# One adaLN part of a diffusion block is multiplied and summed by VectorE instead of TensorE

## The chip, the core and the metric

The kernel runs on one core of a Trainium2 chip. The metric is the device time of one execution in microseconds. The engines are named as in the profile: PE is TensorE, PEld its weight load, DVE is VectorE, ACT is ScalarE, POOL is GpSimd, and SP is the engine whose queue issues nearly all loads from memory.

## The reference, cut to what matters

One block with two sub-layers works on 256 latent tokens and 256 context tokens of width 2048. Each sub-layer is modulated by adaLN: a vector `c` goes through silu and one large matrix, and the result is cut into six vectors of 2048.

```python
def ada_modulation(cond, w, b):
    m = jax.nn.silu(cond) @ w + b          # w: 2048 x 12288
    return jnp.split(m[..., None, :], N_MOD, axis=-1)

sh_a, sc_a, g_a, sh_m, sc_m, g_m = ada_modulation(c, w_ada[layer], b_ada[layer])
h = modulate(rms_norm(x, norm_attn_w), sh_a, sc_a)      # h * (1 + scale) + shift
q, k, v, u = split_projection(h @ w_in)                 # the input projection
...                                                     # rotary, windowed attention, pooling mixer
x = x + g_a * (concat([attn, pool]) @ w_out)
hm = modulate(rms_norm(x, norm_mlp_w), sh_m, sc_m)      # needs sh_m and sc_m
x = x + g_m * squared_relu_mlp(hm, w_up, w_down)
```

The change touches how the first 256 columns of `sc_m` and the first 256 of `sh_m` are computed. They are first read by the MLP, long after the place where they are computed.

## The kernel before, in words

All weights pass once through five buffers `raw` of 128 x 4 x 512 floats (1 MB each). `WeightStream` loads them on SP's queue in a fixed order, each as soon as its buffer is free. There are two kinds of tile. A weight tile ("w") is split in two halves: ACT casts a half to `hi` (L97), DVE subtracts to get `lo` (L98), and PE multiplies in three products (L288 to L290). An adaLN tile ("ada") is read as it lies: its 512 columns are 256 of a scale and 256 of a shift, and four tiles (kg = 0 to 3) cover the 2048 rows of the sum.

The program runs through stages: the first norm, the input projection in five groups of rows, the attention with the pooling mixer beside it, the output projection, the second norm and the MLP. A scheduler with a model of the time chooses each engine's order; every engine then works through its own order strictly.

The adaLN parts that are needed late are spread over these stages. `ADA_LATE` (L32 to L36) lists twelve of them with the engine for each, four steps a part. The first entry, `("m", 0)`, has its four steps in the last group of the input projection (`LATE_IN` = 4), between the products for the values (`ps_v`) and those for the queries (`ps_qu`).

There are two ways to do a part. With "pe" (`ada_pe`) a step is four matmuls (L305), each of 32 columns of `c_sil` against 512 columns of the tile, into a bank `ps_ada`; after the fourth step ACT copies the bank to `ada_e` (L311). With "dve" (`ada_dve`) a step is four VectorE operations over 128 x 512: each multiplies a slice of the tile by a scalar per partition and adds what is there so far (L327; the very first only multiplies, L325). In both ways a finishing step then sums over partitions by small matmuls (`ada_cols`) and adds bias and weight (L340 to L344).

Around the place of the change stand these steps. The last products of the input projection are added to `ka`, `va`, `qa` and `ua` by DVE (L436). Keys and queries are rotated: DVE shuffles a copy (L634), POOL multiplies the copy and the original by the rope table (L635, L636), DVE adds the two (L637). Keys are split by ACT and DVE (L647 to L650). Queries are split for a pair of heads: ACT casts to `qs` (L659), DVE subtracts (L660). The attention works in 16 units; a unit's scores are three matmuls for each of two heads (L717 to L720), its maxima are DVE's (L728 to L730), its exponentials ACT's (L736), and the division is DVE's and ACT's (L740 to L744). The four `ua` groups (`u2` and `u3` of the last input group) are still multiplied between the first units.

Of the kernel before, what the change touches and what calls it, by code (L numbers as in the profile page):

```python
# [8 lines left out]
F32 = mybir.dt.float32  # L9
# [6 lines left out]
P = 128  # L16
# [13 lines left out]


ADA_LATE = (  # L32
    ("m", 0, "pe"), ("m", 1, "pe"),
    ("g", 0, "pe"), ("g", 1, "pe"), ("g", 2, "pe"), ("g", 3, "pe"),
    ("m", 2, "dve"), ("m", 3, "dve"), ("m", 4, "dve"), ("m", 5, "pe"), ("m", 6, "dve"), ("m", 7, "dve"),
)  # L36
# [88 lines left out]
def kernel(  # L125
# [10 lines left out]
    const = ctx.enter_context(tc.tile_pool(name="const", bufs=1, side="left"))  # L136
# [131 lines left out]
    def rstd(pool, ss, n, rest=EPS):  # L268

        nv = pool.tile([P, n], F32, tag="rs_v", name="rs_v", bufs=2)  # L270
        y = pool.tile([P, n], F32, tag="rs_y", name="rs_y", bufs=2)
        u = pool.tile([P, n], F32, tag="rs_u", name="rs_u", bufs=2)
        nc.vector.tensor_scalar(nv, ss, 1.0 / D, rest, ALU.mult, ALU.add)
        nc.vector.tensor_scalar(u.bitcast(I32), nv.bitcast(I32), 1, None, ALU.logical_shift_right)
        nc.vector.tensor_scalar(y.bitcast(I32), u.bitcast(I32), -1, 0x5F3759DF, ALU.mult, ALU.add)
        nc.vector.tensor_scalar(nv, nv, -0.5, None, ALU.mult)
        for _ in range(3):
            for c_ in range(n):
                yc, uc = y[:, c_ : c_ + 1], u[:, c_ : c_ + 1]
                nc.vector.scalar_tensor_tensor(uc, yc, nv[:, c_ : c_ + 1], yc, ALU.mult, ALU.mult)  # L280
            for c_ in range(n):
                yc, uc = y[:, c_ : c_ + 1], u[:, c_ : c_ + 1]
                nc.vector.scalar_tensor_tensor(yc, uc, 1.5, yc, ALU.add, ALU.mult)
        return y
# [30 lines left out]
    def ada_dve(finish):  # L315

        box = {}

        def step(kg):
            raw = S.next("ada")  # L320
            for j in range(4):
                sc = c_sil[:, 4 * kg + j, 0:1]
                if kg == 0 and j == 0:
                    box["e"] = mp.tile([P, 512], F32, tag="ada_v", name="ada_v", bufs=1)
                    nc.vector.tensor_scalar(box["e"], raw[:, j, :], sc, None, ALU.mult)  # L325
                else:
                    nc.vector.scalar_tensor_tensor(box["e"], raw[:, j, :], sc, box["e"], ALU.mult, ALU.add)  # L327

        return [lambda kg=kg: step(kg) for kg in range(4)] + [lambda: finish(box["e"])]

    def ada_cols(e, weights):

        ps = bank("ps_adac")
        for j in range(4):
            nc.tensor.matmul(ps[:, 2 * j : 2 * j + 2], e[:, 128 * j : 128 * j + 128], weights, start=True, stop=True)
        return ps[:, 0:8].rearrange("p (j s) -> p j s", s=2)
# [177 lines left out]
    def late_steps():  # L514
        for what, j, engine in ADA_LATE:
            ada, weights, spread = (ada_pe, sel, selb) if engine == "pe" else (ada_dve, ones[:, 0:2], ones)

            def finish(e, what=what, j=j, weights=weights, spread=spread):
                if what == "m":
                    k = slice(2 * j, 2 * j + 2)  # L520
                    ps = ada_cols(e, weights)
                    ada_scale(am[:, k], ps[:, 0:2], bcol[:, 64 + 2 * j : 66 + 2 * j], cols[:, 48 + 2 * j : 50 + 2 * j])
                    ada_shift(sm[:, k], ps[:, 2:4], bcol[:, 48 + 2 * j : 50 + 2 * j])
                else:
                    ps = bank("ps_g")
                    nc.tensor.matmul(ps, spread, e, start=True, stop=True)
                    gs = gate["a"][:, 512 * j : 512 * j + 512]
                    nc.vector.tensor_tensor(gs, ps, gs, ALU.add)

            steps = ada(finish)  # L530
            yield from steps[:4]
            late_finish.append(steps[4])
# [290 lines left out]
    mp = ctx.enter_context(tc.tile_pool(name="mp", bufs=1, side="right", reuse_waits="tile"))  # L823
# [150 lines left out]
    for b in range(7):  # L974
        acts = early[0:2] if b == 0 else [early[2], up_group()] if b == 1 else [up_group(), up_group()]
        steps = ada_dve(lambda e, b=b: gate_m_chunk(b, e)) if b < 4 else None
        for dg in range(4):
            pss = down_group(b, dg, acts)
            for i in range(2):
                accumulate(y[dg][:, i, :], pss[i], b == 0)  # L980
            if steps:
                steps[dg]()
                if dg == 3:
                    steps[4]()
# [29 lines left out]
    def finish(i, ts, last):  # L1014

        n = 3 + len(ts)
        nc.vector.tensor_reduce(mean[:, i : i + 1], ss3[:, i, 0:n], axis=AX.X, op=ALU.add)
        nc.vector.tensor_scalar(mean[:, i : i + 1], mean[:, i : i + 1], 1.0 / D, EPS, ALU.mult, ALU.add)
        ts.append(last())
        r = rstd(yp, ss3[:, i, n : n + 1], 1, mean[:, i : i + 1])  # L1020
        w = D - 1536
        for h, t in enumerate(ts):
            s = slice(1536 + w // len(ts) * h, 1536 + w // len(ts) * (h + 1))
            nc.vector.scalar_tensor_tensor(x2[:, i, s], t, r, fw[:, s], ALU.mult, ALU.mult)
        for q, eng in ((3, nc.sync), (0, nc.sync), (1, nc.scalar), (2, nc.sync)):
            xs = x2[:, i, 512 * q : 512 * q + 512]
            if q < 2 or q == 2 and i == 0:
                nc.scalar.activation(xs, xs, AF.Copy, scale=r)
            elif q == 2:
                nc.vector.tensor_scalar(xs, xs, r, None, ALU.mult)  # L1030
            eng.dma_start(out=out[P * i : P * i + P, 512 * q : 512 * q + 512], in_=xs)
# [70 lines left out]
```

## Time and profile before

| | us |
|---|---|
| median of 3 runs | 1147.65 |
| lowest and highest run | 1146.72, 1148.39 |
| the profiled execution | 1147.05 |
| its span in the trace | 1145.3 |
| PE busy in the span | 1104.6 (96%) |
| DVE busy | 779.2 (68%) |
| ACT busy | 523.6 (46%) |
| POOL busy | 37.0 (3%) |

The profiled execution took 1.75 us more than its span, and lies 0.60 us under the median. The busy shares are averages over stages with different limits: which engine is late at the place of the change has to be read there.

### The profile page before, as it was taken

What the parts mean: (1) busy time and instruction counts of PE and PEld (TensorE: products, weight loads), DVE (VectorE), ACT (ScalarE), POOL (GpSimd) and SP (SyncE); (2) the same over time, 40 slices, a digit from 0 to 9 for tenths busy, and PEclk for the clock granted to TensorE, in tenths of its full rate; (3) what the DMA queues carried; (4) which work ended last, traced back from release to release, by engine and by line L of the source; (5) the groups of instructions that cost most, each with busy time, mean ns of one, the idle gap of its engine ahead of it and who ended that gap; (6) DMA issues with size and microseconds to landing.
All of it is one profiled execution on the core that took longest, in us unless ns stands there. A gap on an engine that the chain in (4) does not pass through costs nothing.

```text
span 1145.3 us, 16131 instructions
## 1 busy us (share of the span) xinstructions
PE 1104.6 (96%) x6364; PEld 909.3 (79%) x6364; DVE 779.2 (68%) x1222; ACT 523.6 (46%) x796; POOL 37.0 (3%) x53
## 2 busy tenths in 40 slices
PE   4999999999999989999999999999999999999996
PEld 2767778856588869888888888888888888888885
DVE  4655567875588988696774874884664565587576
ACT  4633233499734343365343443433444443443452
POOL 1000001610000000000000000000000000000000
PEclk9999999999999989899999999999999999999998
DMA  9999898687799989977775776775566556566532
GB/s 343 359 341 336 288 325 264 210 292 259 267 369 314 325 306 332 336 246 259 262 265 184 257 269 195 253 267 192 184 192 202 194 184 185 191 192 204 184 110 75
DMA packets 174013, 286.66 MB, mean 250 GB/s; under 512 B 5608, under 2 KB 72352, under 8 KB 172784
## 3 DMA queue, kind: packets, MB, share of 16 engines
q1 hardware_dynamic: 172800, 279.55, 72.9%
q0 software_dynamic: 848, 5.55, 1.3%
q8 instruction: 50, 0.82, 0.3%
q10 hardware_dynamic: 288, 0.52, 0.1%
q14 instruction: 27, 0.22, 0.1%
HBM read 283.50 MB, written 2.10 MB: 249 GB/s over the span
## 4 chain that ended last, share of the span: by engine, by line
PE 88%; DVE 4%; ACT 3%; DMA 3%; issue 1%; SPq 0%; ACTq 0%; DVEq 0%
PE ps_up L919 25%; PE ps_d L288 10%; PE ps_d L289 10%; PE ps_d L290 10%; PE ps_ada L305 4%; PE ps_w L288 3%; PE ps_w L290 3%; PE ps_w L289 3%; PE ps_qu L288 2%; PE ps_qu L290 2%; PE ps_qu L289 2%; PE ps_up L288 1%; DVE lo L98 1%; PE ps_o L763 1%; PE ps_up L289 1%; PE ps_up L290 1%
## 5 line engine op out<-in xcount | busy, mean ns | idle before, releaser
L98 DVE TENSOR_TENSOR lo<-raw,hi 128x1024 fp32r<-128x1024 f32 x330 | 397.7, 1226 | 211.8 <-ACT hi L97 201.0
L97 ACT CAST hi<-raw 128x1024 fp32r<-128x1024 f32 x330 | 338.1, 1050 | 409.1 <-PE ps_up L919 151.7
L919 PE MATMUL ps_up<-mx,hi 128*128 128x512 f32 x832 | 200.1, 393 | 0.0
L288 PE MATMUL ps_d<-hi,ahi 128*128 128x512 f32 (+1 forms) x520 | 200.0, 386 | 0.0
L289 PE MATMUL ps_d<-lo,ahi 128*128 128x512 f32 (+1 forms) x520 | 200.0, 386 | 0.0
L290 PE MATMUL ps_d<-hi,alo 128*128 128x512 f32 (+1 forms) x520 | 198.7, 386 | 0.0
L919 PEld LDWEIGHTS ps_up<-mx,hi 128*128 128x128 f32 x832 | 153.4, 188 | 31.8 <-issue 1.9
L290 PEld LDWEIGHTS ps_d<-hi,alo 128*128 128x128 f32 x520 | 97.7, 188 | 19.8
L288 PEld LDWEIGHTS ps_d<-hi,ahi 128*128 128x128 f32 x520 | 97.7, 188 | 19.5
L289 PEld LDWEIGHTS ps_d<-lo,ahi 128*128 128x128 f32 x520 | 97.7, 188 | 19.3
L919 PEld LDWEIGHTS ps_up<-mx,lo 128*128 128x128 f32 x832 | 106.7, 191 | 4.0
L327 DVE SCALAR_TENSOR_TENSOR ada_v<-raw,c_sil,ada_v 128x512 f32<-128x512 f32 x135 | 100.9, 748 | 12.7 <-DMA raw<-in_w_ada_dram 11.1
L919 PE MATMUL ps_up<-mx,lo 128*128 128x256 f32 x832 | 107.9, 283 | 0.0
L288 PE MATMUL ps_qu<-hhi,hi 128*128 128x256 f32 x240 | 69.3, 290 | 1.4 <-ACT hi L97 1.4
L305 PE MATMUL ps_ada<-raw,c_sil 128*32 128x512 f32 x480 | 68.3, 628 | 2.2 <-DMA raw<-in_w_ada_dram 1.9
L290 PE MATMUL ps_qu<-hhi,lo 128*128 128x256 f32 x240 | 67.0, 282 | 0.3 <-DVE lo L98 0.3
L289 PE MATMUL ps_qu<-hlo,hi 128*128 128x256 f32 x240 | 66.9, 280 | 0.0
L288 PEld LDWEIGHTS ps_qu<-hhi,hi 128*128 128x128 f32 x240 | 45.1, 188 | 16.6 <-issue 8.4
L288 PE MATMUL ps_up<-mx,hi 128*128 128x256 f32 x192 | 54.7, 293 | 1.8 <-ACT mx L884 1.5
L289 PE MATMUL ps_up<-mx,hi 128*128 128x256 f32 x192 | 54.3, 287 | 0.0
L290 PE MATMUL ps_up<-mx,lo 128*128 128x256 f32 x192 | 53.1, 287 | 0.4 <-DVE lo L98 0.4
L288 PE MATMUL ps_w<-hi,mx 128*128 128x512 f32 x128 | 50.4, 395 | 0.0
(202 smaller groups left out, 1336.4 us busy)
## 6 DMA issues: line engine op xcount, KB each, us to landing
raw<-in_w_ada_dram SPq DMA_DIRECT2D x128, 512.0 KB, 7.3
raw<-in_w_mlp_up_dram SPq DMA_DIRECT2D x64, 1024.0 KB, 5.5
raw<-in_w_mlp_down_dram SPq DMA_DIRECT2D x64, 1024.0 KB, 5.1
raw<-in_w_ada_dram SPq DMA_DIRECT2D x32, 1024.0 KB, 6.8
raw<-in_w_in_dram SPq DMA_DIRECT2D x19, 1024.0 KB, 7.6
raw<-in_w_out_dram SPq DMA_DIRECT2D x16, 1024.0 KB, 7.5
xnat<-in_x_dram SPq DMA_DIRECT2D x2, 1024.0 KB, 6.0
xnat<-in_ctx_dram SPq DMA_DIRECT2D x2, 1024.0 KB, 11.7
```

The lines of the kernel that those rows point to most:

```text
L97: up = nc.scalar.copy(hi, raw)
L98: low = nc.vector.tensor_tensor(lo, raw, hi.bitcast(F32), ALU.subtract)
L288: nc.tensor.matmul(ps, a[0], b[0], start=first, stop=False, skip_group_check=True)
L289: nc.tensor.matmul(ps, a[0], b[1], start=False, stop=False, skip_group_check=True)
L290: nc.tensor.matmul(ps, a[1], b[0], start=False, stop=last, skip_group_check=True)
L305: nc.tensor.matmul(ps[32 * j : 32 * j + 32, :], c_sil[:, 4 * kg + j, :], raw[:, j, :], start=(kg == 0), stop=(kg == 3), tile_position=(0, ...
L327: nc.vector.scalar_tensor_tensor(box["e"], raw[:, j, :], sc, box["e"], ALU.mult, ALU.add)
L763: nc.tensor.matmul(ps[64 * i : 64 * i + 64, 0:T], va[k // 2][:, k % 2, 64 * g : 64 * g + 64], pT[:, k, i, :], start=(k == 0), stop=(k == 3 ...
L919: nc.tensor.matmul(ps, wk, h, start=part == k == 0, stop=part == 1 and k == KC - 1, skip_group_check=True)
```

## The change

The first entry of `ADA_LATE` goes from "pe" to "dve". Its sixteen products and sums are issued on DVE in place of sixteen matmuls on PE. The pool `mp`, where `ada_dve` keeps its sum, isn't open yet at this place, so the constant tile `ada_e` is used there. The copy of the bank by ACT goes; the sum over partitions uses `ones` in place of `sel`.

```diff
 ADA_LATE = (
-    ("m", 0, "pe"), ("m", 1, "pe"),
+    ("m", 0, "dve"), ("m", 1, "pe"),
...
                 if kg == 0 and j == 0:
-                    box["e"] = mp.tile([P, 512], F32, tag="ada_v", name="ada_v", bufs=1)
+                    if mp:
+                        box["e"] = mp.tile([P, 512], F32, tag="ada_v", name="ada_v", bufs=1)
+                    else:
+                        box["e"] = const.tile([P, 512], F32, tag="ada_e", name="ada_e", bufs=1)
                     nc.vector.tensor_scalar(box["e"], raw[:, j, :], sc, None, ALU.mult)
...
         return [lambda kg=kg: step(kg) for kg in range(4)] + [lambda: finish(box["e"])]
+
+    mp = None
```

Lines from L326 on stand three lines further down in the changed kernel, and those from L329 on five: the multiplying step L325 and the adding step L327 are L328 and L330 there, and the accumulation L436 is L441.

The scheduler orders the engines anew. On DVE, at the end of the input projection, this stands before, from the rotation of the second query block (`qa_272`) to the maxima of the first unit; `qa_271` to `qa_274` are the four query blocks, `qs_2108` and `qs_2111` the split queries of the first two heads, which the first two units read, and `lo` belongs to the tile that `u3` multiplies:

```order
L634 STREAM_SHUFFLE rot<-qa_272 128x2x256
L637 TENSOR_TENSOR qa_271<-qa_271,rot 128x512
L98 TENSOR_TENSOR lo<-raw,hi 128x1024 x2
L660 TENSOR_TENSOR qs_2108<-qa_271,qs_2108 64x256
L436 TENSOR_TENSOR qa_273<-ps_qu,qa_273 128x512
L660 TENSOR_TENSOR qs_2111<-qa_271,qs_2111 64x256
L660 TENSOR_TENSOR qs_2166<-qa_271,qs_2166 64x256
L637 TENSOR_TENSOR qa_272<-qa_272,rot 128x512
L660 TENSOR_TENSOR qs_2169<-qa_271,qs_2169 64x256
L634 STREAM_SHUFFLE rot<-qa_273 128x2x256
L436 TENSOR_TENSOR qa_274<-ps_qu,qa_274 128x512
L728 TENSOR_REDUCE st<-ps_s 128x1 x2
```

and now, in the same place (`qs_2106` and `qs_2109` are the split queries of the first two heads here):

```order
L330 SCALAR_TENSOR_TENSOR ada_e<-raw,c_sil,ada_e 128x512
L441 TENSOR_TENSOR qa_274<-ps_qu,qa_274 128x512
L639 STREAM_SHUFFLE rot<-qa_272 128x2x256
L639 STREAM_SHUFFLE rot<-qa_273 128x2x256
L642 TENSOR_TENSOR qa_271<-qa_271,rot 128x512
L330 SCALAR_TENSOR_TENSOR ada_e<-raw,c_sil,ada_e 128x512
L639 STREAM_SHUFFLE rot<-qa_274 128x2x256
L665 TENSOR_TENSOR qs_2106<-qa_271,qs_2106 64x256
L330 SCALAR_TENSOR_TENSOR ada_e<-raw,c_sil,ada_e 128x512
L665 TENSOR_TENSOR qs_2109<-qa_271,qs_2109 64x256
L665 TENSOR_TENSOR qs_2164<-qa_271,qs_2164 64x256
L642 TENSOR_TENSOR qa_272<-qa_272,rot 128x512
```

The last four adding steps of the part stand among the rotation and the splitting of the queries (the fourth of them follows two rows further down), and the shuffles of `qa_273` and `qa_274` and the accumulation of `qa_274` have moved ahead of the first split queries. POOL's order is the same: four products of 128 x 256 for the keys and eight of 128 x 512 for the queries, each pair behind its shuffle.

On PE, among the products for the values, this stands before:

```order
L290 MATMUL ps_v<-hi,hlo 128x256
L288 MATMUL ps_v<-hi,hhi 128x256
L289 MATMUL ps_v<-lo,hhi 128x256
L290 MATMUL ps_v<-hi,hlo 128x256
L305 MATMUL ps_ada<-raw,c_sil 32x512 x4
L288 MATMUL ps_v<-hi,hhi 128x256
L289 MATMUL ps_v<-lo,hhi 128x256
```

and now:

```order
L290 MATMUL ps_v<-hi,hlo 128x256
L288 MATMUL ps_v<-hi,hhi 128x256
L289 MATMUL ps_v<-lo,hhi 128x256
L290 MATMUL ps_v<-hi,hlo 128x256
L288 MATMUL ps_v<-hi,hhi 128x256
L289 MATMUL ps_v<-lo,hhi 128x256
```

The four matmuls of a step are gone, at this and at three more places, and the products around them are in the order that they had.

## Rows read from the trace of the kernel before

**Rows 1.** The page's part 4: shares of the chain that ended last.

```profile
PE 88%; DVE 4%; ACT 3%; DMA 3%; issue 1%; SPq 0%; ACTq 0%; DVEq 0%
```

**Rows 2.** Windows: start:end, length, busy of each engine, granted clock, DMA share, GB/s.

```profile
173.40:206.40 33.00, 33.00 (x249) 27.84 (x248) 26.16 (x42) 14.21 (x21) 9.51 (x8) 1.00 0.84 276
206.40:212.70 6.30, 5.36 (x41) 4.99 (x41) 6.11 (x13) 0.00 (x0) 2.16 (x2) 1.00 0.94 318
212.70:230.00 17.30, 17.30 (x131) 13.36 (x129) 14.25 (x33) 11.25 (x27) 13.65 (x18) 1.00 0.39 129
230.00:280.00 50.00, 46.95 (x325) 27.57 (x324) 34.33 (x92) 47.23 (x115) 4.07 (x5) 1.00 0.73 258
408.00:414.70 6.70, 6.70 (x34) 2.34 (x37) 6.67 (x20) 3.31 (x8) 0.00 (x0) 0.50 0.41 123
```

**Rows 3.** Timeline of PE around the first step: start, length, then the idle time before.

```profile
187.32 0.28 PE L290 MATMUL ps_v<-hi,hlo 128*128 128x256 f32 x1
187.53 1.06 PE L305 MATMUL ps_ada<-raw,c_sil 128*32 128x512 f32 x8
...
188.75 0.28 PE L289 MATMUL ps_v<-lo,hhi 128*128 128x256 f32 x1
```

**Rows 4.** Timeline of PE at the first scores, and behind a later stall.

```profile
206.87 0.50 PE L717 MATMUL ps_s<-khi,qs 128*128 128x512 f32 x1 [0.46 <-DVE qs L660]
...
208.13 0.47 PE L717 MATMUL ps_s<-khi,qs 128*128 128x512 f32 x1 [0.48 <-DVE qs L660]
...
208.74 0.33 PE L288 MATMUL ps_qu<-hhi,hi 128*128 128x256 f32 x1
...
221.35 0.22 PE L720 MATMUL ps_s<-mask_r,ident_r 128*128 128x128 f32 x1
...
407.11 0.70 PE L868 MATMUL ps_r<-diag,ones 128*128 128x256 f32 x2 [2.92 <-DVE diag L866]
```

**Rows 5.** Timeline of DVE from the query weights to the third unit's maxima.

```profile
194.81 2.36 DVE L98 TENSOR_TENSOR lo<-raw,hi 128x1024 fp32r<-128x1024 f32 x2 [0.45 <-ACT hi L97]
...
201.20 0.69 DVE L637 TENSOR_TENSOR qa<-qa,rot 128x512 f32<-128x512 f32 x1
202.54 3.83 DVE L98 TENSOR_TENSOR lo<-raw,hi 128x1024 fp32r<-128x1024 f32 x2 [0.65 <-ACT hi L97]
...
207.57 0.87 DVE L660 TENSOR_TENSOR qs<-qa,qs 64x256 fp32r<-64x256 f32 x2
...
212.72 0.37 DVE L729 SCALAR_TENSOR_TENSOR st<-st,nsink 128x2 f32<-128x2 f32 x1
...
224.22 1.28 DVE L728 TENSOR_REDUCE st<-ps_s 128x1 f32<-128x512 f32 x2
225.54 1.05 DVE L729 SCALAR_TENSOR_TENSOR st<-st,nsink 128x2 f32<-128x2 f32 x1
```

**Rows 6.** Timeline of POOL: products of the rotation, and one of the pooling mixer.

```profile
199.88 1.28 POOL L636 TENSOR_TENSOR qa<-qa,rope 128x512 f32<-128x512 f32 x1
201.22 1.83 POOL L635 TENSOR_TENSOR rot<-rot,rope 128x512 f32<-128x512 f32 x1
203.01 2.28 POOL L636 TENSOR_TENSOR qa<-qa,rope 128x512 f32<-128x512 f32 x1
...
225.49 1.09 POOL L671 TENSOR_TENSOR win<-win 128x538 f32<-128x538 f32 x1
```

**Rows 7.** Timeline of DVE in the output projection, where parts are already DVE's.

```profile
351.92 0.75 DVE L327 SCALAR_TENSOR_TENSOR ada_v<-raw,c_sil,ada_v 128x512 f32<-128x512 f32 x1
352.58 1.22 DVE L98 TENSOR_TENSOR lo<-raw,hi 128x1024 fp32r<-128x1024 f32 x1
```

**Rows 8.** Timeline of SP: loads of the part's four tiles, two for each.

```profile
162.38 4.38 SPq L84 DMA_DIRECT2D raw<-in_w_ada_dram  x4
...
169.77 5.49 SPq L84 DMA_DIRECT2D raw<-in_w_ada_dram  x4
```

**Rows 9.** Timeline of ACT in the third and fourth unit.

```profile
225.67 1.34 ACT L744 ACTIVATE p<-p,st 128x512 f32<-128x512 f32 x2 [2.66 <-DVE st L741]
```

## The prediction

> **What bounds the kernel now.** I read the chain that ended last first: PE holds 88% of it and DVE 4% [rows 1]. That says that removed PE work is time gained where PE leads, and it doesn't say where that is. So I cut the place of the change into windows [rows 2]. From 173.40 to 206.40, the end of the input projection, PE is busy for 33.00 of 33.00 us. DVE is busy for 26.16 us there, so 6.84 us of it are free. From 206.40 to 212.70 the order of things turns: DVE is busy for 6.11 of 6.30 us and PE for 5.36. PE's two waits there are for DVE's splits of the first queries, 0.46 and 0.48 us [rows 4]. So before the change the two engines come to the first scores almost together, DVE a little later. From 212.70 to 230.00 PE leads again (17.30 of 17.30), and from 230.00 ACT (47.23 of 50.00, PE 46.95).
>
> **What is removed.** Four steps of four matmuls leave PE. Around the first step the products for the values go from 187.32 to 188.75 [rows 3]. Two products in a row without a step between take about a quarter of a microsecond of that, so a step costs 1.2 us and four cost 4.8. The three other steps look the same. PE would then stand at the first scores at about 201.6 in place of 206.4. ACT's copy of the bank goes too; ACT is busy for 14.21 of 33.00 us up to 206.40 [rows 2], nothing waits behind it, and I count it at nothing.
>
> **What is added, without contention.** The part is sixteen operations of 128x512 on DVE. Where the kernel already has them, one starts 0.66 us before the operation behind it [rows 7]. In the new order fifteen of the sixteen stand ahead of the second split of queries, on which PE's second scores wait. Fifteen times 0.66 is 9.9 us; the very first only multiplies and may be a little cheaper, which I leave. Two shuffles and one accumulation move ahead of that split as well. I take 0.69 us for each, from the addition of the same size [rows 5], together 2.1. So 12.0 us more must pass through DVE's queue before PE can go on.
>
> Against it stand 6.84 us of free time [rows 2]. I let all of it be filled, which is generous, since some of it is time in which DVE waits for PE or ACT and will wait again. Before the change DVE also lost time at 202.54, where two subtractions took 3.83 us in place of 2.36 at 194.81 [rows 5]; those 1.5 us I take out here, because I count such losses by themselves below. So without contention the split ends 12.0 - 6.8 - 1.5 = 3.7 us later. It ended at about 208.0, half way through the row at 207.57 [rows 5]; now at 211.7.
>
> That is already the main finding. PE comes 4.8 us earlier to a point at which it must wait until a time that is later than before. The 4.8 us turn into waiting.
>
> **What is added by contention.** At 201.20 an addition on DVE and a product on POOL begin together. The product takes 1.83 us, where the one before took 1.28 [rows 6], and its end at 203.05 is that of a product that began when the addition was over (201.20 + 0.69). Then the two subtractions of DVE and the next product meet: DVE loses 1.5 us and the product takes 2.28. They take turns, whole instructions at a time. A tiny operation shows it too: the scalar-tensor-tensor of 128x2 took 1.05 us at 225.54, while a sum on POOL ran from 225.49 to 226.58 [rows 5, 6]; alone it took 0.37.
>
> In the old order few of DVE's operations met a product. In the new one DVE has no gaps, so every product that falls ahead of the second split of queries costs its length, unless DVE is at an operation which reads only one operand from SBUF (a shuffle, or an accumulation from PSUM). By the order on POOL and DVE, seven of the query products fall there: two for each of three query blocks and the first of the fourth, since the four shuffles now stand ahead. Seven times 1.28 is 9.0 us; one accumulation and two shuffles lie beside them, 2.1 off: 6.9. The four key products are half the size, 0.64 each, 2.6 together; an accumulation and a small operation hide 0.8 of it: 1.8. So contention costs 8.7 us and the split ends at 220.4, 12.4 later than before.
>
> The bounds of this term are nothing (no turns between the adding steps and POOL) and 11.6 us (each of the eleven products in full). I take 8.7, because the rows nearest to it, subtraction and addition of the same kind of operands, show turns each time they meet.
>
> No row shows an adding step of this size beside a POOL product. The Trainium skill (SBUF — State Buffer, section "SBUF: two separate sides") has one pair of ports that VectorE and GpSimd share, held for a whole instruction, and a VectorE instruction with two SBUF inputs is among those that hold it. By that rule, with which the subtraction at 202.54 agrees, the adding steps take turns with the rope products; without it the time would be that of the first rival below. It speaks against putting this part beside the rotation.
>
> **What becomes of the delay.** Three things follow. First, PE restarts 12.4 us late. Second, some of it is taken back: the third unit's scores were done on PE at 221.57 [rows 4], but its maxima started on DVE only at 224.22 [rows 5], and ACT was idle for 2.66 us there [rows 9]. With PE later, DVE has done its work by then, so I take 2.7 us off. Third, PE's clock. After an idle time of 2.92 us that ended at 407.11 [rows 4] the granted clock was 0.50 (1.2 of 2.4 GHz) over 408.00 to 414.70 [rows 2]: 6.7 us at half speed, 3.35 us of work lost. The new idle time is longer, about 10 to 19 us. PE leads after it until ACT takes over, so I count half, 1.7 us, with nothing and 3.35 as the ends. Sum: 12.4 - 2.7 + 1.7 = 11.4.
>
> **Transfers.** SP's order stays, but the buffers of the part's four tiles come free by DVE's steps in place of PE's. All four tiles' loads were issued between 162.38 and 175.26 [rows 8], ahead of nearly all of DVE's steps, so those hardly wait for data. The load that takes the last tile's buffer starts up to 16 us later than before (about 222 in place of 206). Its reader on PE stands 11 us later as well and several products behind; I count nothing, with up to 4 us if that cover is gone. Nothing is queued on SP that is read sooner. In the stages behind, PE leads and the delay passes to the end.
>
> **The sum.** 1147.05 for the profiled execution plus 11.4 is 1158.45. That execution lies 0.60 under the median, so I forecast 1159.0, slower.
>
> **Rivals.**
>
> The adding steps don't take turns with POOL, and only subtractions and additions do. For it: no row shows such a step of this size beside a POOL product. Against it: the tiny one at 225.54. In the order, an adding step stands opposite to three query products and about two key products, some 5 us of the 8.7. The split then ends at 215.4, 7.4 later; 7.4 - 2.7 + 1.7 = 6.4, so 1154.1.
>
> No contention at all, or a scheduler's order in which the products happen to fall beside accumulations: 3.7 us at the split. With 2.7 taken back and half the clock's loss that is +2.7, 1150.3; where the clock costs nothing it is +1.0, 1148.6. This is also the case in which the change is not seen.
>
> The other side: DVE's queue has room and PE's 4.8 us reach the end, 1142.9. It decides if the second split of queries ends before 203.3, that is 4.8 earlier than now. DVE's free time up to there would have to hold all 12 us, and it has 6.84. What speaks for it is only that later stages take back more than I see: the units are led by ACT from 230.00 on, where PE is idle for 3.05 of 50 us [rows 2]. That isn't enough to take back 12.
>
> **Chances.** The forecast with contention: 0.60. The first rival: 0.12. No contention: 0.18, of which 0.09 is within 0.2%. The faster one: 0.07. A larger delay, from a late tile or a longer loss at the lower clock: 0.03. About 0.2% (2.3 us) is what a measurement of this kernel can tell from no change. So faster 0.07, within it 0.09, slower 0.84. The range runs from 1148.5, which keeps the most part of the case without contention, to 1163.5, which is 12.4 us and the clock's 3.35 with nothing taken back (1147.65 + 15.75 = 1163.4).
>
> **What would show it right or wrong.** In the changed profile PE should come to the first scores near 201.6, and wait there for DVE's split of queries, in two waits that sum to between 10 and 19 us. DVE should have almost no idle time from 176 on until the first maxima. Some adding steps among the rotations should take about 1.3 us more than 0.75, or POOL's rope products more than 1.28. The granted clock should be 0.50 for a few microseconds behind the wait. The third unit's maxima should follow their scores at once. I am wrong if PE's wait at the scores is under 4.8 us (then the change gains), if the adding steps beside POOL's products keep their 0.75 us (then the first rival holds), or if PE is late by 12 us at 230 and on time at 400 (then a later stage has slack that I didn't find).

## The result and the profile after

| | before | after |
|---|---|---|
| median of the runs beside each other, us | 1148.02 (4 runs) | 1158.74 (4 runs) |
| the same, measured again | 1147.16 (17 runs) | 1160.92 (5 runs) |
| ratio, 95% interval | | 1.0102 [1.0079, 1.0125] |
| the same, measured again | | 1.0115 [1.0092, 1.0138] |
| profiled execution, and its span | 1147.05, 1145.3 | 1162.85, 1161.1 |

The change costs 1.0 to 1.2%, 11 to 14 us. Executions of one kernel differ by 3 to 10 us here, and the profiled one of the changed kernel is the longest of its four; a second profile (run "after_again") has a span of 1157.4 us. Up to the end of the attention the two agree within 0.4 us, so the rows below are from the first, and stages behind are compared with the second too.

The windows of the changed kernel, to be set beside [rows 2] (the same columns):

```profile
173.40:206.40 33.00, 27.98 (x217) 26.70 (x216) 32.44 (x53) 12.24 (x16) 7.93 (x6) 0.96 0.82 274
206.40:212.70 6.30, 0.00 (x0) 0.00 (x0) 6.30 (x10) 1.61 (x4) 4.36 (x4) 0.50 0.49 166
212.70:230.00 17.30, 14.25 (x93) 12.54 (x94) 14.74 (x26) 5.47 (x11) 9.95 (x11) 0.77 0.23 71
230.00:280.00 50.00, 47.27 (x327) 28.98 (x326) 34.49 (x89) 43.47 (x105) 9.86 (x13) 1.00 0.80 287
```

In the first window DVE (the third of the five engines) went from 26.16 to 32.44 us of 33.00, and PE fell from 33.00 to 27.98. In the second DVE has no gap, PE does nothing, and the granted clock is 0.50.

The timeline of PE at the first scores, to be set beside [rows 4]:

```profile
213.99 0.79 PE L722 MATMUL ps_s<-khi,qs 128*128 128x512 f32 x1 [12.61 <-DVE qs L665]
...
217.07 0.80 PE L722 MATMUL ps_s<-khi,qs 128*128 128x512 f32 x1 [1.76 <-DVE qs L665]
...
218.20 0.52 PE L288 MATMUL ps_qu<-hhi,hi 128*128 128x256 f32 x1
...
421.27 1.22 PE L873 MATMUL ps_r<-diag,ones 128*128 128x256 f32 x2 [2.91 <-DVE diag L871]
```

PE was ready at 201.4 and waited 12.61 and 1.76 us for DVE's splits of queries. The second scores start at 217.07 in place of 208.13.

DVE's timeline in that wait, and POOL's (beside [rows 5] and [rows 6]); L330 is the adding step, L641 and L640 are the rope products:

```profile
205.91 1.75 DVE L330 SCALAR_TENSOR_TENSOR ada_e<-raw,c_sil,ada_e 128x512 f32<-128x512 f32 x1
...
210.78 1.75 DVE L330 SCALAR_TENSOR_TENSOR ada_e<-raw,c_sil,ada_e 128x512 f32<-128x512 f32 x1
...
213.97 1.65 DVE L330 SCALAR_TENSOR_TENSOR ada_e<-raw,c_sil,ada_e 128x512 f32<-128x512 f32 x1
215.65 2.79 DVE L665 TENSOR_TENSOR qs<-qa,qs 64x256 fp32r<-64x256 f32 x2
...
219.64 0.75 DVE L330 SCALAR_TENSOR_TENSOR ada_e<-raw,c_sil,ada_e 128x512 f32<-128x512 f32 x1
```

```profile
204.86 2.24 POOL L641 TENSOR_TENSOR qa<-qa,rope 128x512 f32<-128x512 f32 x1
...
210.27 1.71 POOL L641 TENSOR_TENSOR qa<-qa,rope 128x512 f32<-128x512 f32 x1
...
213.62 1.45 POOL L641 TENSOR_TENSOR qa<-qa,rope 128x512 f32<-128x512 f32 x1
215.03 1.71 POOL L640 TENSOR_TENSOR rot<-rot,rope 128x512 f32<-128x512 f32 x1
```

The step at 205.91 ends at 207.66, 0.56 us behind the end of the product that began at 204.86. The one at 219.64 meets no product and takes 0.75. Two splits that took 0.87 us before [rows 5] take 2.79.

The third unit, to be set beside its scores and maxima in [rows 4] and [rows 5]:

```profile
231.89 0.22 PE L725 MATMUL ps_s<-mask_r,ident_r 128*128 128x128 f32 x1
...
233.20 0.68 DVE L733 TENSOR_REDUCE st<-ps_s 128x1 f32<-128x512 f32 x1
```

The times of a trace count from its first instruction, and the runs don't reach the place of the change equally soon. A step of DVE that stands ahead of the change in every run, the bias of an earlier part (`am_a`), shows it, here before, after and in the run short_rope below:

```profile
173.46 0.16 DVE L340 TENSOR_TENSOR am_a<-ps_adac,bcol 128x4 f32<-128x4 f32 x1
...
173.51 0.16 DVE L345 TENSOR_TENSOR am_a<-ps_adac,bcol 128x4 f32<-128x4 f32 x1
...
172.43 0.16 DVE L363 TENSOR_TENSOR am_a<-ps_adac,bcol 128x4 f32<-128x4 f32 x1
```

Over all runs it starts between 172.26 and 173.85. The difference is there long before the change (an accumulation into `ka` starts at 95.29 before and at 94.27 in short_rope), so no edit makes it. Delays are therefore counted from this step.

The delay along the program, from the profiles (`am_a`; start of the second scores; ACT's table load ahead of the first exponentials; the last wait of the attention's products on PE; the second norm's `ps_r`; the end):

| run | `am_a` | second scores | first exponentials | end of attention | second norm | span |
|---|---|---|---|---|---|---|
| before | 173.46 | 208.13 | 213.17 | 306.48 | 407.11 | 1145.3 |
| after | 173.51 | 217.07 | 222.94 | 318.46 | 421.27 | 1161.1 |
| after_again | 173.85 | 217.39 | 223.26 | 318.81 | 419.45 | 1157.4 |

Counted from `am_a`, the delay is 8.9 us at the second scores, 9.7 at the exponentials, 11.9 at the end of the attention, and 12 (14 in the longer execution) at the second norm. Up to the end of the attention the two profiles of the changed kernel agree within 0.03 us. At the end nothing of the delay is given back.

### The profile page after: what moved, and what is told of

The parts are those of the page before. It is cut to its first block, busy times and chain, and to the rows that moved or that the text cites. A ratio compares the mean times of both kernels' runs of the same rounds, so it can differ in the third digit from the quotient of the medians.

```text
span 1161.1 us, 16079 instructions
## 1 busy us (share of the span) xinstructions
PE 1104.3 (95%) x6332; PEld 910.8 (78%) x6332; DVE 793.6 (68%) x1238; ACT 523.5 (45%) x795; POOL 39.7 (3%) x53
## 4 chain that ended last, share of the span: by engine, by line
PE 72%; DVE 11%; DMA 11%; ACT 4%; issue 2%; SPq 1%; ACTq 0%; DVEq 0%
PE ps_up L924 25%; PE ps_d L289 10%; PE ps_d L290 10%; PE ps_d L288 10%; DMA raw<-in_w_out_dram 4%; DMA raw<-in_w_mlp_up_dram 4%; PE ps_ada L305 4%; DVE lo L98 3%; DVE ada_v L330 2%; PE ps_qu L288 2%; PE ps_qu L290 2%; DMA raw<-in_w_ada_dram 2%; PE ps_qu L289 2%; ACT hi L97 1%; PE ps_o L768 1%
## 5 line engine op out<-in xcount | busy, mean ns | idle before, releaser
L330 DVE SCALAR_TENSOR_TENSOR ada_v<-raw,c_sil,ada_v 128x512 f32<-128x512 f32 x135 | 100.9, 747 | 21.2 <-DMA raw<-in_w_ada_dram 19.7
L305 PE MATMUL ps_ada<-raw,c_sil 128*32 128x512 f32 x448 | 64.4, 625 | 1.8 <-DMA raw<-in_w_ada_dram 1.8
```

What stands on the lines that cost most here:

```text
L305: nc.tensor.matmul(ps[32 * j : 32 * j + 32, :], c_sil[:, 4 * kg + j, :], raw[:, j, :], start=(kg == 0), stop=(kg == 3), tile_position=(0, ...
```

## The experiments

Where an edit says "order kept", a table of ranks holds DVE, ACT, POOL and PE to a given order by edges that make no engine wait for another; so an edit changes durations and not the order.

```python
own = [i for i in traced if str(i.engine) == "EngineType." + name]
line = [own[a + k] for a, n in runs for k in range(n)]
for first, then in zip(line, line[1:]):
    tc.add_manual_dep(then, first.name, mybir.DependencyInfo(mybir.DependencyClass.NoSync, mybir.DependencyReason.DATA), reason="order")
```

How much later than in the kernel before each run is, in us, counted from `am_a` (in the kernel before the three places are 34.7, 133.0 and 233.7 us behind it):

| run | `am_a` | second scores | end of attention | second norm |
|---|---|---|---|---|
| after_again | 173.85 | 8.9 | 11.9 | 11.9 |
| short_rope | 172.43 | 2.1 | 6.4 | 6.4 |
| short_steps | 172.69 | 5.0 | 8.8 | 8.9 |
| both | 172.54 | 9.7 | 13.1 | 14.3 |
| short_pe | 172.66 | 0.3 | 1.0 | 1.0 |
| keep_warm | 173.10 | 9.2 | 12.2 | 13.4 |
| later_order | 173.03 | 0.1 | 6.0 | 7.2 |
| former_order | 172.26 | 8.9 | 11.4 | 11.4 |
| late_former | 172.44 | 1.3 | 8.5 | 8.5 |
| short_both | 172.39 | -0.9 | -0.7 | 0.9 |

**The changed kernel again** (after_again), no edit.

> The changed kernel once more, as the measure for the others: 1158.7, ratio 1.0102. In its profile PE restarts the products of u2 9 to 10 us later than in the kernel before, and the difference at the end is 10 to 12 us.

Measured: 1160.92 us, 1.0115. The second scores are 8.9 us late, a little less than expected. The difference at the end is 13.8 us between medians, more than expected, with the first measurement's 10.7 inside the spread.

**Short rope products** (short_rope): the changed kernel, order kept.

```diff
-        nc.gpsimd.tensor_tensor(tmp, tmp, rope[:, 1:2, :].broadcast_to([P, n, T]), ALU.mult)
-        nc.gpsimd.tensor_tensor(t, t, rope[:, 0:1, :].broadcast_to([P, n, T]), ALU.mult)
+        few = slice(0, 8)
+        nc.gpsimd.tensor_tensor(tmp[:, :, few], tmp[:, :, few], rope[:, 1:2, few].broadcast_to([P, n, 8]), ALU.mult)
+        nc.gpsimd.tensor_tensor(t[:, :, few], t[:, :, few], rope[:, 0:1, few].broadcast_to([P, n, 8]), ALU.mult)
```

> The changed kernel, every engine in its order, but POOL's rope products run over 16 of 512 columns (that part of the rotation is left out). Theory (DVE's queue and the turns with POOL): DVE's second split of queries ends about 8 us earlier than in the changed kernel, PE restarts the products of u2 near 210.5 in place of 218.2, and the time falls from 1158.7 to about 1150 to 1152. Rival (no turns; DVE is late by its own work alone, the long operations beside POOL are an artefact of the records): PE restarts within 2 us of 218.2 and the time stays at 1157 to 1159.

Measured: 1154.04 us, 1.0061 [1.0048, 1.0074]. The timeline of PE:

```profile
207.91 0.80 PE L741 MATMUL ps_s<-khi,qs 128*128 128x512 f32 x1 [7.62 <-DVE qs L684]
...
209.17 0.79 PE L741 MATMUL ps_s<-khi,qs 128*128 128x512 f32 x1
```

and of DVE:

```profile
206.02 0.74 DVE L348 SCALAR_TENSOR_TENSOR ada_e<-raw,c_sil,ada_e 128x512 f32<-128x512 f32 x1
...
207.89 0.77 DVE L348 SCALAR_TENSOR_TENSOR ada_e<-raw,c_sil,ada_e 128x512 f32<-128x512 f32 x1
208.69 0.87 DVE L684 TENSOR_TENSOR qs<-qa,qs 64x256 fp32r<-64x256 f32 x2
```

The adding steps, of full size, are back at 0.75 us and the two splits at 0.87; the second scores start 6.8 us earlier than in after_again, counted from `am_a`. The sum of what DVE's operations up to the split on which these scores wait took longer in the changed kernel than here is 6.8 us too; 3.8 us of it fall on five adding steps, the rest on subtractions, an addition and the splits. So the turns with POOL are shown, and their size at this place was 6.8 against 8.7 in the sum. The time is 2 us above the 1150 to 1152 expected: of the 6.8 us 5.6 are left at the end of the attention; where the rest went is the matter of the order runs below.

**Short adding steps** (short_steps): the changed kernel, order kept.

```diff
-                    nc.vector.scalar_tensor_tensor(box["e"], raw[:, j, :], sc, box["e"], ALU.mult, ALU.add)
+                    few = slice(0, 512 if mp else 8)
+                    nc.vector.scalar_tensor_tensor(box["e"][:, few], raw[:, j, few], sc, box["e"][:, few], ALU.mult, ALU.add)
```

> The changed kernel, every engine in its order, but fifteen of the sixteen adding steps run over 8 of 512 columns (that part of the sum is left out). Theory: with the steps' time gone DVE keeps only the moved shuffles and accumulation (2 us) and their turns with POOL, PE restarts at 207 to 210 and the time is 1146 to 1150, about that of the kernel before; PE's 4.8 us still don't come through. Rival 1 (the new order itself is what costs): 1154 or more. Rival 2 (PE's 4.8 us come through as soon as DVE has room): 1143.

Measured: 1156.24 us, 1.0082 [1.0064, 1.0099]. In number that is rival 1's, but the new order is only a part of it (see the order runs): the second scores already start 5.0 us later than before. The timeline of DVE says why:

```profile
206.96 1.22 DVE L349 SCALAR_TENSOR_TENSOR ada_e<-raw,c_sil,ada_e 128x8 f32<-128x8 f32 x1
...
209.70 1.12 DVE L349 SCALAR_TENSOR_TENSOR ada_e<-raw,c_sil,ada_e 128x8 f32<-128x8 f32 x1
210.85 2.87 DVE L684 TENSOR_TENSOR qs<-qa,qs 64x256 fp32r<-64x256 f32 x2
...
214.93 0.23 DVE L349 SCALAR_TENSOR_TENSOR ada_e<-raw,c_sil,ada_e 128x8 f32<-128x8 f32 x1
```

A step over 8 columns takes 0.23 us alone and 1.12 to 1.22 beside a product: it lasts until the product under way ends, however short DVE's operation is. The step at 206.96 ends at 208.18, and POOL's product is this one:

```profile
206.44 1.71 POOL L660 TENSOR_TENSOR qa<-qa,rope 128x512 f32<-128x512 f32 x1
```

The run took away the steps' own time, worth 3.9 us at the second scores (some of it DVE now spends waiting for PE, 2.74 us at 183.81), and left the turns. My expectation had overlooked that.

**PE's steps put back** (both): the changed kernel; DVE, ACT and POOL in order kept.

```diff
             raw = S.next("ada")
+            if not mp:
+                if kg == 0:
+                    box["ps"] = bank("ps_ada")
+                for j in range(4):
+                    nc.tensor.matmul(
+                        box["ps"][32 * j : 32 * j + 32, :], c_sil[:, 4 * kg + j, :], raw[:, j, :],
+                        start=(kg == 0), stop=(kg == 3), tile_position=(0, 32 * j),
+                    )
```

> The changed kernel with PE's sixteen matmuls of the part put back beside DVE's steps (into a bank that nobody reads); DVE, ACT and POOL in the order of the changed kernel. Theory: PE's 4.8 us are worth nothing, since PE waits 14 us behind them; the wait gets 4.8 us shorter and the time stays within 1.5 us of the changed kernel's 1158.7. Rival (part of PE's saving reached the end): up to 1163.5.

Measured: 1160.68 us, 1.0117 [1.0101, 1.0133]. That is 2.0 us above 1158.7 and so just outside the expected 1.5, but the time of after_again (1160.92). PE's first wait is 8.26 us in place of 12.60, and the second scores start 0.8 us later than in after_again: DVE gets its input later from a PE that has more to do. So of the 4.8 us that PE saved 0.8 reached the scores, and the times show nothing of it.

**PE's steps shortened in the kernel before** (short_pe), order kept; `few` is 32 for this part.

```diff
-                    ps[32 * j : 32 * j + 32, :], c_sil[:, 4 * kg + j, :], raw[:, j, :],
+                    ps[32 * j : 32 * j + 32, 0 : (few if kg else 512)], c_sil[:, 4 * kg + j, :], raw[:, j, 0 : (few if kg else 512)],
```

> The kernel before, every engine in its order, but twelve of the sixteen matmuls of the part run over 32 of 512 columns (that part of the sum is left out), so that PE has about 3.3 us less to do before the first scores and DVE has nothing new. Theory: DVE's queue is nearly as late as PE at the first scores, PE waits longer there, and the gain is 0 to 1.5 us: 1146 to 1148. Rival (PE leads, and what it saves is gained): 1144.5.

Measured: 1146.05 us, 0.9994 [0.9978, 1.0010]. PE is ready 2.8 us earlier, its first wait grows from 0.46 to 3.57 us, and its second scores start no earlier (0.3 us later, counted from `am_a`). Even without any work added to DVE, PE's time here gains nothing that can be told from none; the full 3.3 us (0.9971) lie outside the interval. What holds DVE here is not only its own work:

```profile
193.28 2.00 ACT L97 CAST hi<-raw 128x1024 fp32r<-128x1024 f32 x2 [3.18 <-DMA raw<-in_w_in_dram]
...
200.74 1.78 DVE L655 TENSOR_TENSOR qa<-qa,rot 128x512 f32<-128x512 f32 x1 [1.29 <-POOL qa L654]
```

The tile of weights that ACT waits for came no earlier than in the kernel before (its cast starts 20.6 us behind `am_a`, 20.3 before). Its subtraction, the accumulation and the shuffle on DVE, POOL's products and this addition follow it in a row, ahead of the splits. So in the kernel before the lateness of DVE's queue includes a transfer. In the changed kernel DVE has no gap there, and this transfer doesn't hold it.

**PE kept at work in its wait** (keep_warm): the changed kernel.

```diff
     split_queries(0)
+    keep = bank("ps_keep")
+    for n in range(100):
+        nc.tensor.matmul(keep[:, 0:T], ident_r, mask_r.rearrange("p a b -> p (a b)"), start=True, stop=True)
```

> The changed kernel with 100 matmuls of 128x256 into a bank that nobody reads, on PE right ahead of the first scores, where it waits 12.6 us. Theory: the granted clock stays at 1.00 through the first scores and the products behind; in the changed kernel it was 0.50 up to 220.7, of which 2.5 us of products and the second scores lay on the path, so the time falls by 1 to 2 us, to about 1157. Rival (the units behind are led by DVE and ACT anyway): no difference, 1158.7.

Measured: 1.0111 [1.0098, 1.0125], no difference, but the run doesn't decide. Windows of PE (granted clock is the third number from the right):

```profile
206.00:212.90 6.90, 6.90 (x58) 6.74 (x57) 6.90 (x10) 1.62 (x4) 4.93 (x4) 1.00 0.47 152
...
214.50:217.00 2.50, 0.11 (x2) 0.03 (x1) 2.44 (x3) 0.00 (x0) 2.50 (x3) 0.69 0.00 0
...
220.00:222.00 2.00, 2.00 (x11) 2.00 (x11) 2.00 (x5) 0.00 (x0) 0.00 (x0) 0.50 0.26 50
```

The clock stayed at 1.00 (2.4 GHz) through the first wait, fell to 0.50 in the second, of 2.39 us, and stayed there to 222, where it had come back by 220.7 in the changed kernel. The lower clock was moved, not taken away. What it costs at the end stays open.

**Two other parts moved** (m5_dve, m1_dve): the kernel before with one other entry changed. The first pair of lines is m1_dve, written against the changed kernel, the second m5_dve against the kernel before; the order is the scheduler's in both.

```diff
-    ("m", 0, "dve"), ("m", 1, "pe"),
+    ("m", 0, "pe"), ("m", 1, "dve"),
...
-    ("m", 2, "dve"), ("m", 3, "dve"), ("m", 4, "dve"), ("m", 5, "pe"),
+    ("m", 2, "dve"), ("m", 3, "dve"), ("m", 4, "dve"), ("m", 5, "dve"),
```

> The kernel before with another part moved, the sixth for the MLP's scale and shift, whose steps lie in the first groups of the MLP: DVE sums it in place of PE. There PE is busy for 90 of 93 us, DVE for 78 of 93, and POOL does nothing. Theory: 10.6 us of steps fit into DVE's free 15 us only in part, but nothing takes turns with POOL; PE's 4.8 us come through at least in half: 1143 to 1146. Rival (DVE's subtractions come late for PE's products): 1149 to 1152.

> The kernel before with the second part moved in place of the first: its steps lie among the first units of the attention, where POOL sums for the pooling mixer (busy 13.65 of 17.30 us) and DVE is busy for 14.25 of 17.30. Theory: turns with POOL and no room on DVE again make PE or ACT wait for maxima and splits: 1151 to 1157. Rival (what counts is only that DVE is late before the first scores, and behind them there is room): 1143 to 1148.

Measured: m5_dve 1160.84 us, 1.0119 [1.0096, 1.0142], and m1_dve 1161.40 us, 1.0122 [1.0099, 1.0145], both about as slow as the change. PE's longest new wait in m5_dve, then those of m1_dve (the first a second one for the steps' sum):

```profile
430.79 1.87 PE L335 MATMUL ps_adac<-ones,ada_v 128*128 128x2 f32 x8 [11.15 <-DVE ada_v L327]
```

```profile
230.78 1.97 PE L757 MATMUL tp_p<-ident,p 128*128 128x128 f32 x8 [5.79 <-ACT p L749]
...
250.95 1.87 PE L340 MATMUL ps_adac<-ones,ada_e 128*128 128x2 f32 x8 [5.45 <-DVE ada_e L330]
```

For m5_dve neither expectation held: there was no turn with POOL and no late subtraction ahead of PE's products. PE's own small matmuls that finish the part stood in its order 11 us before DVE's sum was ready, and PE doesn't pass them. For m1_dve the theory had the direction and its waits, but the time is 4 us above its range.

**The order of the attention alone** (later_order, former_order): the kernel before, and the changed kernel, each in its own order to the first unit's scores and maxima and in the other's order behind; nothing is left out.

> The kernel before, with PE's steps, in its own order up to the first unit's scores and maxima; behind them DVE, ACT and PE work in the order of the changed kernel. In the traces of the runs with the new order the stretch from the restart behind the first scores to the second norm is 200.9 to 203.4 us long, in the kernel before and with shortened PE steps 198.4 to 199.0. Theory (the new order of the attention itself costs): that stretch is 2.5 to 5 us longer here too, and the time is 1149.5 to 1152. Rival (the stretch is longer only because the units start late): no difference, 1147.

> The changed kernel in its own order up to the first unit's scores and maxima; behind them DVE, ACT and PE work in the order of the kernel before. Theory (the new order of the attention costs): 2.5 to 4 us less than the changed kernel's 1158.7 to 1160.9, so about 1157. Rival (it is the late start that makes the attention longer): no difference, 1159 to 1161.

Measured: later_order 1153.74 us, 1.0049 [1.0030, 1.0069], and former_order 1157.88 us, 1.0090 [1.0071, 1.0109]. With the units starting on time (second scores at 207.79) the new order costs 5.9 us up to the end of the attention: 104.3 us from the second scores, where before has 98.3. With the late start the former order has 100.9 and the new one 101.4. So the new order is a real cost where the start is not late; in the changed kernel the former order would have taken off only 0.5 us of the extra 3. The two lose their time at different places. In the former order the delay is 9.3 us at the third unit's exponentials and 9.8 at the sixteenth's, and most of the rest comes at the end; in the new order it grows from 8.7 to 11.9 between these units, and no more comes at the end. The intervals of former_order and the changed kernel overlap, so a gain from the former order isn't shown. ACT in former_order waits at the end of the attention for a transfer (0.42 us there in the kernel before):

```profile
311.67 1.99 ACT L97 CAST hi<-raw 128x1024 fp32r<-128x1024 f32 x2 [1.99 <-DMA raw<-in_w_out_dram]
```

**Eight steps moved back** (late_former): as former_order, with this on DVE behind the first maxima in place of among the rotations and splits:

```order
L753 TENSOR_TENSOR st<-sink,st 128x2
L348 SCALAR_TENSOR_TENSOR ada_e<-raw,c_sil,ada_e 128x512 x8
L459 TENSOR_TENSOR ua_275<-ps_qu,ua_275 128x2x256
```

> As the run with the former order of the attention (1157.9), but the last eight of the sixteen adding steps stand on DVE right behind the first unit's maxima in place of among the key splits, the rotation and the query splits; nothing is left out. Theory (the steps beside the rotation and ahead of the splits are what makes PE wait): PE's second scores start at 208 to 210 in place of 215.8, of which 3 to 4 us are given back because the second unit's maxima stand behind the eight steps: 1150 to 1153. Rival (DVE has too much to do around here wherever the steps stand): 1156 to 1158.

Measured: 1155.25 us, 1.0080 [1.0052, 1.0109], above the expectation and not to be told from former_order. The trace decides half of it:

```profile
208.42 0.80 PE L740 MATMUL ps_s<-khi,qs 128*128 128x512 f32 x1
...
222.01 1.02 PE L358 MATMUL ps_adac<-ones,ada_e 128*128 128x2 f32 x8 [4.19 <-DVE ada_e L348]
```

The second scores start at 208.42, 7.6 us earlier than in former_order when counted from `am_a`, as the theory says. Then the eight steps (6.26 us in a row) stand ahead of the first unit's division and the second unit's maxima, ACT waits 4.42 us and PE 4.19 for the sum, and at the end of the attention 2.9 us are left of the 7.6. At neither of the two places is the work free for DVE.

**DVE without both** (short_both): as former_order, with the edits of short_rope and short_steps together.

> As the run with the former order of the attention, but POOL's rope products run over 16 of 512 columns and fifteen adding steps over 8 of 512 (those parts of the rotation and the sum are left out): DVE has room before the first scores. Theory (PE's saving is real and was only covered by DVE): PE's second scores start 3 to 5 us earlier than in the kernel before (208.1), near 204, and the time is 1142 to 1145. Rival (the saving is lost later in any case, in the units that ACT leads): 1147.

Measured: 1148.50 us, 1.0009 [0.9996, 1.0023], nearer the rival's time. The second scores start 0.9 us earlier than before, not 3 to 5. In this order DVE still has the moved shuffles and the accumulation ahead of them, and PE's wait there is still for DVE (4.81 us). The exponentials are 1.4 to 2.1 us earlier in all sixteen units, so little is lost in these. It goes behind them, where ACT waits 1.22 us for the output weights (0.42 before) and PE restarts at a granted clock of 0.52 over 304.70 to 308.00 (1.00 at this place before):

```profile
304.75 1.08 PE L788 MATMUL ps_o<-pT,va 128*64 128x256 f32 x2 [1.05 <-ACT pT L779]
305.76 0.80 PE L306 MATMUL ps_w<-hi,mx 128*128 128x512 f32 x1
```

At the second norm the run is 0.9 us later than before, so the theory's gain is not shown.

## Why the prediction was right

It forecast 1159.0 in a range of 1148.5 to 1163.5, slower; measured were 1158.74 and 1160.92. The main finding held: PE's time becomes waiting, and DVE's new work and its turns with POOL make the first scores late. The size of the total came right in part by luck, since the terms were off in opposite directions.

- **What bounds the place.** Right in the main. DVE and PE come to the first scores together, and PE's work there is worth little by itself: short_pe (0.9994) and both (1.0117 against 1.0115). That DVE's lateness before the change includes a transfer (short_pe) I had not seen.
- **PE's 4.8 us.** Right in size: PE was ready at 201.4, forecast 201.6. Right in effect: they became waiting, 14.4 us in two waits, forecast 10 to 19.
- **DVE's queue without contention.** 3.7 us was too high. In short_rope, where next to nothing takes turns, the second scores start 2.1 us later than before. I had 12.0 us of new work less 8.3 of room, and the room was larger. Part of it, 0.8 us by the run both, is that DVE gets its input from a PE that is 4.8 us earlier, which I left out when I called the use of all idle time generous. The other 0.8 us are not accounted for.
- **Contention.** 8.7 us forecast, 6.8 by short_rope. Adding steps beside a product of the queries took 1.65 to 1.75 us, forecast about 2.0 (0.75 and 1.3), since each met a product that had begun; shuffles and an accumulation beside products kept their length (0.72 at 212.46, 0.68 at 203.69), as forecast. The rule of the Trainium skill (SBUF — State Buffer, section "SBUF: two separate sides") that I set beside the row is borne out for this instruction: the trace agrees, with 1.75 us beside a product and 0.74 to 0.77 where the products are short. The first rival, in which adding steps take no turns, falls: 3.8 of the 6.8 us are theirs. One reading was wrong: the tiny operation's 0.37 us at 212.72 was not its time alone, as POOL's product that began at 211.79 was still under way; alone it takes 0.15 (at 222.71 in the changed kernel). That makes its 1.05 at 225.54 a stronger sign of turns.
- **The end of the split.** 220.4 forecast (12.4 late), about 217.0 measured (8.9 late): the sum of the two terms above.
- **What is given back.** Here a step failed. I took off 2.7 us, since the third unit's maxima had started 2.65 us behind the end of their scores. In the changed kernel they start 1.1 us behind it (232.11 and 233.20), so some 1.5 us were given back there, and at this unit's exponentials the delay is 8.7 us. What failed is that the rest would pass on as it is, PE leading the stages behind. The whole order behind is made anew, and by the sixteenth unit's exponentials the delay is 11.9 us. From the second scores to the end of the attention the changed kernel took 3 us more, where I had 1.0 us less (2.7 off, 1.7 for the clock).
- **The clock.** 0.50 from within the wait to 220.7, as forecast. On PE it cost the 1.7 us of the sum: from the second scores to the thirteenth product behind them went 3.73 us (217.07 to 220.80), where it had been 2.07 (208.13 to 210.20). How much of it reached the end is not separated from the 3 us above (keep_warm).
- **Transfers.** Counted at nothing with 4 us as the bound. For the first output weights ACT waits 0.53 us in after_again and 0.42 before, so nothing in the changed kernel; in former_order, as late but in the other order, it waits 1.99.
- **The sum.** 12.4 - 2.7 + 1.7 = 11.4 forecast; 8.9 and some 3 measured, 11.9 at the second norm of after_again. That is luck: 3.5 us too much at the splits met 4 us too little behind them.

The rival on the other side, faster by 4.8, needed the second split to end before 203.3. No run brought that about: short_both gave DVE much room and still had its second scores at 206.19. What an earlier split would be worth at the end stays open; the 1.4 to 2.1 us that short_both gained in the units were lost before the second norm.

## What to carry to other kernels

Before moving work from the engine that is busiest overall, look at the stretch itself: here PE was busy for 33 of 33 us and its work was still worth next to nothing, because a second engine came to the same meeting point at the same time. An operation on VectorE with two operands from SBUF cost its own length plus what was left of the GpSimd operation that it met, here about 1 us each time for a step beside a product of the queries; count the meetings in the order, not the bytes. A delay that is found at one point should not be reduced by slack seen further on unless the work that uses the slack is named; in a scheduled kernel the order behind changes too, and that alone was worth 6 us in one run. And before comparing the times of two traces, look for a step ahead of the change that both have: here it differed by up to 1.6 us.

## What the runs showed of the hardware that I had not expected

A turn between VectorE and GpSimd costs the short one the rest of the long one: an operation over 8 columns, 0.23 us alone, took 1.12 to 1.22 us and ended within 0.03 us of the product that it met. And the granted clock of TensorE fell without a long wait. In keep_warm PE was at work at 1.00 for 12 us, waited 0.88 us, worked for 0.8 us, waited 2.39 us and restarted at 0.50. In short_both it restarted at 0.50 at 304.75, and the two waits just ahead were 0.78 and 1.05 us long; before the change, with a wait of 1.06 us at that place and none just ahead of it, the clock kept 1.00.
